# Final norm of token tiles 2 and 3: product and row scaling in one VectorE operation

## The chip, the cores and the metric

The kernel runs on one core of one Trainium2 chip. The metric is the device time of one execution in microseconds; the median of several executions is compared. The core has five engines with a queue of instructions each: TensorE (PE, matmuls), VectorE (DVE), ScalarE (ACT), GpSimd (POOL) and SyncE (SP, which here only issues DMA transfers). ScalarE and GpSimd issue transfers too. An engine runs its queue in order and waits where an instruction needs another engine's result.

## The reference

One layer of a decoder block on 512 tokens with a width of 1024: conditioning from `c`, a combined input projection, two mixers, their merge, a SwiGLU feed-forward layer, and a last RMS norm. All in fp32. The end of it, which the change touches:

```
    h2 = rms_norm(x, norm2_g) * (1.0 + scale2) + shift2
    f_g, f_u = jnp.split(h2 @ w_ffn_in, 2, axis=-1)
    x = x + gate2 * ((jax.nn.silu(f_g) * f_u) @ w_ffn_out)
    return rms_norm(x, final_norm_g)

def rms_norm(x, g):
    y = x * lax.rsqrt(jnp.mean(x * x, axis=-1, keepdims=True) + EPS)
    return y * g
```

## The kernel before

The 512 tokens are four tiles of 128 rows, `xt[0]` to `xt[3]` (`xr` in the profile), with 1024 columns each. Instructions are written out in the order in which each engine runs them; the compiler adds the waits. So the order of the lines is the order of every queue.

The last matrix product, of the gated activations with `w_ffn_out`, is computed by a Strassen-like scheme: seven products of half-size blocks are accumulated in PSUM banks (`pfo`). `zprod` (L1751) runs one such product over six chunks of weights. For each chunk, `get` (L144) first prepares the chunk two ahead: ScalarE copies the raw weights to a rounded high part (`hi`, L112), VectorE subtracts it to get the low part (`lo`, L116), and SP loads a further chunk (L92). Then come the side tasks given for the chunk, then TensorE's matmuls, three for each pair of blocks (L53 to L55).

When the sums of a block of tokens are complete, it is added to the residual stream. `resid_v` (L1234) multiplies a PSUM bank by the gate (`rt`, L1238), adds it to `xt` (L1239), and returns a function that squares the result on ScalarE and accumulates the squares of each row into `ss2` (L1240). In the kernel before, `res_` (L1818) follows this with `scale_g` (L1724), a VectorE product of the new columns of `xt` with the gain vector `fng` into `xo` (L1730).

The last product in time gives tiles 0 and 1, so tiles 2 and 3 are complete earlier. Their three remaining blocks of 512 columns are added during the first three chunks of `zprod(1, "S4", ...)` (L1834). In between stand the weight splits for the last three chunks. Then `done(2)` and `done(3)` finish those rows:

- `row_rstd` (L1246): VectorE adds up the row's squares (L1247), GpSimd raises the sum to the power -1/2 (L1248), into the column `r2[:, tk]` (`sm` in the profile);
- `finish` (L1732): ScalarE scales the last 384 columns of `xo` by that column (L1733), VectorE the first 640 (L1734), and ScalarE and SP each issue a transfer of their part to the output.

After that comes the loop over tiles 0 and 1 (L1842): 15 matmuls for tile 0, twice 15 of half width for tile 1, each followed by residual add, product with the gain, sum, power, scaling and output. The last row's sum is taken in another way (L1864 to L1867). A copy of half a bank on ScalarE (L1836) precedes the loop.

Of the kernel before, what the change touches and what calls it, by code (L numbers as in the profile page):

```python
# [12 lines left out]
AF = mybir.ActivationFunctionType  # L13
OP = mybir.AluOpType
# [3 lines left out]
D = 1024  # L18
# [10 lines left out]
def block_kernel(ctx: ExitStack, tc: tile.TileContext, x, positions, w_ada, b_ada, w_in,  # L29
# [3 lines left out]
    T, V, A, P, SY = nc.tensor, nc.vector, nc.scalar, nc.gpsimd, nc.sync  # L33
# [4 lines left out]
    x, out = x[0], out[0]  # L38
# [3 lines left out]
    def bank(k, name="bank"):  # L42
        return psum.tile([128, 512], F32, name=name, tag=f"b{k}", bufs=1)
# [100 lines left out]
    def get(i, ahead=2):  # L144
        k = wseq.index(i)
        ensure(wseq[min(k + ahead, len(wseq) - 1)])
        return chunk[i]
# [180 lines left out]
    xt = []  # L328
# [903 lines left out]
    r2 = sm[:, 16:20]  # L1232

    def resid_v(p, c0, n, slot, tk, gate):  # L1234

        cs_ = slice(c0, c0 + n)
        t = t512("rt")
        V.tensor_mul(t[:, :n], p, gate[:, cs_])  # L1238
        V.tensor_add(xt[tk][:, cs_], xt[tk][:, cs_], t[:, :n])  # L1239
        return lambda: A.activation(t[:, :n], xt[tk][:, cs_], AF.Square, scale=1.0 / 32,  # L1240
                                    accum_out=ss2[:, tk, slot:slot + 1])
# [4 lines left out]
    def row_rstd(tk):  # L1246
        V.tensor_reduce(r2[:, tk:tk + 1], ss2[:, tk], op=OP.add, axis=AX.X)  # L1247
        P.tensor_tensor(r2[:, tk:tk + 1], r2[:, tk:tk + 1], mhalf[:, :1], op=OP.pow)  # L1248
# [393 lines left out]
    for q in range(-2, NQ):  # L1642
        g, u = 2 + q // 2, q % 2
# [78 lines left out]
    xo = []  # L1722

    def scale_g(c0, n, tk):  # L1724
        if not xo:
            for k in range(2):
                t = ffn[0].tile([128, 2, D], F32, name="xo", tag=f"E{k + 1}", bufs=1)
                xo.extend((t[:, 0], t[:, 1]))
        cs_ = slice(c0, c0 + n)
        V.tensor_mul(xo[tk][:, cs_], xt[tk][:, cs_], fng[0][:, cs_])  # L1730

    def finish(tk):  # L1732
        A.activation(xo[tk][:, 640:], xo[tk][:, 640:], AF.Copy, scale=r2[:, tk:tk + 1])  # L1733
        V.tensor_scalar(xo[tk][:, :640], xo[tk][:, :640], r2[:, tk:tk + 1], None, op0=OP.mult)  # L1734
        for c, q in ((slice(0, 640), SY), (slice(640, 1024), A)):
            q.dma_start(out[tk * 128:(tk + 1) * 128, c], xo[tk][:, c])
# [4 lines left out]
    def zmm(o, ka, c, e, w, cc, start, stop):  # L1741
        ah, al = za[ka, c // 2 if c < 5 else 3]
        wh, wl = w
        for j in range(1 + (c < 5)):
            k_ = 2 * (c % 2) + j if c < 5 else 0
            a = tuple(t[:, k_, e * 128:(e + 1) * 128] for t in (ah, al))
            mm3(o, a, (wh[:, j, cc], wl[:, j, cc]), start and j == 0, stop, skip_group_check=True)
# [3 lines left out]
    def zprod(k, ka, kw, start, tasks):  # L1751
        if start:
            Z[k] = [bank(ZB[k][e], "pfo") for e in range(2)]
        for c, i in enumerate(W_Z[kw][:len(tasks)]):
            w = get(i)
            for fn in tasks[c]:
                fn()
            for e in range(2):
                zmm(Z[k][e], ka, c, e, w, ALL, start and c == 0, c == NZ - 1)
# [29 lines left out]
    fng = []  # L1789
# [25 lines left out]

    sq = []

    def res_(tk, h):  # L1818
        def fn():
            sq.append(resid_v((Z[h] if tk < 2 else Z[2 + h])[tk % 2], 512 * h, 512, h, tk, gate_b[2]))  # L1820
            scale_g(512 * h, 512, tk)
        return fn

    def sq_():
        while sq:
            sq.pop(0)()

    zprod(2, "A22", 4, False, [[res_(0, 0)], [sq_, res_(1, 0)], [sq_], [res_(2, 1)], [sq_, hi_("S4", 3)], [lo_("S4", 3)]])

    def done(tk):  # L1830
        row_rstd(tk)
        finish(tk)

    zprod(1, "S4", (1, 1), False, [[res_(3, 1)], [sq_, res_(2, 0)], [sq_, res_(3, 0)]])  # L1834
    last = bank(7, "pfo")
    A.activation(last[:, :256], Z[1][1][:, 256:], AF.Copy)  # L1836
    ids = W_Z[1, 1][3:]
    ch = [get(i, 2 - k) for k, i in enumerate(ids)]
    sq_()
    done(2)  # L1840
    done(3)
    for tk in range(2):  # L1842
        for z in range(2) if tk else (None,):
            c = ALL if z is None else slice(256 * z, 256 * z + 256)
            o = Z[1][0] if z is None else (Z[1][1][:, :256], last[:, :256])[z]
            for n_, w in enumerate(ch):
                zmm(o, "S4", 3 + n_, tk, w, c, False, n_ == 2)
            n = c.stop - c.start
            if z is None:
                resid(o, 512, 512, 1, tk, gate_b[2])  # L1850
                scale_g(512, 512, tk)
                row_rstd(tk)
            elif z == 0:
                resid(o, 512, n, 1, tk, gate_b[2])
                scale_g(512, n, tk)
                A.activation(xo[0], xo[0], AF.Copy, scale=r2[:, 0:1])
                for c_, q in ((slice(0, 640), SY), (slice(640, 1024), A)):
                    q.dma_start(out[0:128, c_], xo[0][:, c_])

                P.tensor_scalar(ss2[:, tk, 3:4], ss2[:, tk, 1:2], ss2[:, tk, 0:1], EPS, op0=OP.add, op1=OP.add)  # L1860
            else:
                resid_v(o, 768, n, 2, tk, gate_b[2])
                c_ = slice(768, 768 + n)
                V.tensor_tensor_reduce(out=t512("sq")[:, :n], in0=xt[tk][:, c_], in1=xt[tk][:, c_],  # L1864
                                       scale=1.0 / 1024, scalar=ss2[:, tk, 3:4], op0=OP.mult, op1=OP.add,
                                       accum_out=ss2[:, tk, 2:3])
                P.tensor_tensor(r2[:, tk:tk + 1], ss2[:, tk, 2:3], mhalf[:, :1], op=OP.pow)  # L1867
                scale_g(768, n, tk)
                finish(tk)
# [49 lines left out]
```

## Time and profile before

| | us |
|---|---|
| median of 3 runs | 823.59 |
| lowest and highest run | 823.27, 824.55 |
| the profiled execution, its own time | 823.06 |
| span of its instructions | 821.3 |
| TensorE busy | 805.2 (98%) |
| VectorE busy | 688.6 (84%) |
| ScalarE busy | 431.7 (53%) |
| GpSimd busy | 162.3 (20%) |

The span runs from the first to the last instruction; the rest of the execution's time lies around it. Busy times of matmuls overlap, so 98% isn't a measure of how well TensorE is used. TensorE's granted clock was 0.996. A row of the timeline gives start, duration, engine, source line, operation, output and inputs with their shape, and in brackets the idle time before it and what ended it. A row of the chain of waits gives start, duration and the instruction on which the end depends at that moment; "issue" there is time in which the engine waited for nothing that the profile shows.

### The profile page before, as it was taken

Reading aid. Unit: us, or ns where it says so; the run is one execution under the profiler, and the core shown is the slowest. Engines: PE = TensorE matmul, PEld = TensorE weight load, DVE = VectorE, ACT = ScalarE, POOL = GpSimd, SP = SyncE. Lnnn points to the kernel's source line nnn. Section 1 sums busy time; section 2 is a strip of 40 time slices with the busy share of each in tenths; the row PEclk is TensorE's granted clock in tenths of the full one; section 3 lists DMA queues with packets and bytes.
Section 4 is the critical chain, followed back from the end, with each engine's and each line's share of the span. In section 5 each row is a group of like instructions: output and inputs, shape, how many; then the busy total and the mean of one; then the engine's idle time right before and its main releaser. Section 6 shows DMA issues by size and latency. Waiting matters only on the chain.

```text
span 821.3 us, 12948 instructions
## 1 busy us (share of the span) xinstructions
PE 805.2 (98%) x4903; PEld 719.6 (88%) x4903; DVE 688.6 (84%) x1178; ACT 431.7 (53%) x773; POOL 162.3 (20%) x186
## 2 busy tenths in 40 slices
PE   7999999999999999999999999999999999999995
PEld 6889889988888888988888899999999999888874
DVE  7989788898899658887697879889999888897686
ACT  6674445322332226665636586555555556576553
POOL 2060031362354411000010010323121222000001
PEclk9999999999999999999999999999999999999998
DMA  9974352332346553037692603979897977556662
GB/s 294 311 213 119 103 180 78 104 102 86 106 145 204 179 180 103 26 110 256 198 248 43 198 27 117 217 234 275 267 252 208 239 186 192 189 191 202 198 193 113
DMA packets 108462, 141.35 MB, mean 172 GB/s; under 512 B 6688, under 2 KB 77344, under 8 KB 108208
## 3 DMA queue, kind: packets, MB, share of 16 engines
q1 hardware_dynamic: 97296, 110.54, 42.5%
q0 software_dynamic: 10384, 29.17, 15.3%
q8 instruction: 38, 0.62, 0.3%
q10 hardware_dynamic: 720, 0.82, 0.3%
q14 instruction: 24, 0.20, 0.1%
HBM read 138.15 MB, written 25.17 MB: 199 GB/s over the span
## 4 chain that ended last, share of the span: by engine, by line
PE 89%; DVE 5%; DMA 3%; ACT 2%; issue 1%; SPq 0%; POOL 0%; POOLq 0%; ACTq 0%; DVEq 0%
PE pb L53 9%; PE pb L55 9%; PE pb L54 9%; PE R L53 6%; PE R L54 6%; PE R L55 6%; PE pfo L53 4%; PE pfo L55 4%; PE pfo L54 4%; PE pav L54 2%; PE pav L53 2%; PE pav L55 2%; PE pgb L53 2%; PE pgb L54 2%; PE pgb L55 2%; PE po L54 2%
## 5 line engine op out<-in xcount | busy, mean ns | idle before, releaser
L112 ACT ACTIVATE hi<-raw 128x1024 fp32r<-128x1024 f32 (+2 forms) x108 | 109.3, 1013 | 104.0 <-PE pb L54 38.6
L116 DVE TENSOR_TENSOR lo<-raw,hi 128x1024 fp32r<-128x1024 f32 (+2 forms) x72 | 83.5, 1163 | 24.4 <-ACT hi L112 24.1
L116 POOL TENSOR_TENSOR lo<-raw,hi 128x1024 fp32r<-128x1024 f32 x29 | 73.0, 2520 | 127.7 <-ACT hi L112 126.8
L53 PE MATMUL pb<-h,hi 128*128 128x512 f32 (+1 forms) x192 | 74.6, 389 | 0.0
L54 PE MATMUL pb<-h,hi 128*128 128x512 f32 (+1 forms) x192 | 74.0, 385 | 0.0
L55 PE MATMUL pb<-h,lo 128*128 128x512 f32 (+1 forms) x192 | 74.0, 385 | 0.0
L53 PE MATMUL pfo<-hi,za 128*128 128x512 f32 (+1 forms) x144 | 55.9, 388 | 0.3 <-ACT ps L1770 0.3
L55 PE MATMUL pfo<-hi,za 128*128 128x512 f32 (+1 forms) x144 | 55.8, 388 | 0.0
L54 PE MATMUL pfo<-lo,za 128*128 128x512 f32 (+1 forms) x144 | 55.8, 387 | 0.0
L177 DVE SCALAR_TENSOR_TENSOR acc<-mraw,cols,acc 128x512 f32<-128x512 f32 x49 | 40.8, 833 | 17.8 <-DMA mraw<-in_w_ada_dram 16.8
L53 PE MATMUL R<-tb,sx 128*128 128x256 f32 x160 | 45.3, 283 | 0.6 <-ACT R L1689 0.3
L54 PE MATMUL R<-tb,sx 128*128 128x256 f32 x160 | 45.1, 282 | 0.0
L55 PE MATMUL R<-tb,sx 128*128 128x256 f32 x160 | 45.0, 281 | 0.0
L55 PE MATMUL R<-tb,lo 128*128 128x256 f32 x160 | 44.8, 280 | 0.0
L53 PE MATMUL R<-tb,hi 128*128 128x256 f32 x160 | 44.8, 280 | 0.0
L54 PE MATMUL R<-tb,hi 128*128 128x256 f32 x160 | 44.6, 279 | 0.0
L55 PEld LDWEIGHTS pb<-h,lo 128*128 128x128 f32 x192 | 36.0, 187 | 7.3
L54 PEld LDWEIGHTS pb<-h,hi 128*128 128x128 f32 x192 | 36.0, 188 | 6.9
L53 PEld LDWEIGHTS pb<-h,hi 128*128 128x128 f32 x192 | 36.0, 188 | 6.9
L322 POOL COPY sm<-sm 128x1 f32<-128x1 f32 x36 | 23.1, 641 | 86.3 <-ACT sm L321 86.3
L54 PE MATMUL pav<-lo,h 128*128 128x256 f32 x128 | 35.8, 279 | 0.0
L302 POOL DMA_DIRECT2D wsum<-in_w_ffn_out_dram x24 | 21.3, 888 | 73.3 <-DMA wsum<-wsum 42.2
(385 smaller groups left out, 2657.8 us busy)
## 6 DMA issues: line engine op xcount, KB each, us to landing
raw<-in_w_ffn_in_dram SPq DMA_DIRECT2D x44, 512.0 KB, 6.0
raw<-in_w_in_dram SPq DMA_DIRECT2D x40, 512.0 KB, 3.6
wsum<-in_w_ffn_out_dram POOLq DMA_DIRECT2D x30, 512.0 KB, 8.8
mraw<-in_w_ada_dram SPq DMA_DIRECT2D x28, 512.0 KB, 3.8
raw<-wsum SPq DMA_DIRECT2D x20, 512.0 KB, 3.7
raw<-in_w_ffn_out_dram SPq DMA_DIRECT2D x16, 512.0 KB, 4.2
s<-in_w_ada_dram SPq DMA_DIRECT2D x30, 256.0 KB, 5.5
wsum<-wsum POOLq DMA_DIRECT2D x10, 512.0 KB, 5.2
```

What stands on the lines that cost most here:

```text
L53: T.matmul(o, wh, rh, start=start, stop=False, **kw)
L54: T.matmul(o, wh, rlo, start=False, stop=False, **kw)
L55: T.matmul(o, wlo, rh, start=False, stop=stop, **kw)
L112: A.activation(hi[:, :m], e["raw"][:, :m], AF.Copy)
L116: e["lo"].tensor_sub(lo[:, :m], e["raw"][:, :m], f(hi[:, :m]))
L177: V.scalar_tensor_tensor(o, w, cs[:, j:j + 1], o, op0=OP.mult, op1=OP.add)
L302: P.dma_start(wsum[n][o], src, accum_op=OP.add)
L322: P.tensor_copy(t, t)
```

## The change

It concerns tiles 2 and 3 only. For the one block of tile 2 and the two blocks of tile 3 that are added during the last product, the product with the gain vector right after the residual add is left out. After the last weight split both rows' sums and powers are asked for, one after the other. Then a new function, `scaled`, finishes each tile: VectorE multiplies `xt` by the row's column and by the gain vector in one operation, 512 columns for tile 2 and 1024 for tile 3. The other 512 columns of tile 2 have their product already, and ScalarE scales them. Each tile goes out in two transfers of 512 columns, one from SP and one from ScalarE. Tiles 0 and 1 are finished as before.

```diff
+    def scaled(tk, n):
+
+        if n < D:
+            A.activation(xo[tk][:, n:], xo[tk][:, n:], AF.Copy, scale=r2[:, tk:tk + 1])
+        V.scalar_tensor_tensor(xo[tk][:, :n], xt[tk][:, :n], r2[:, tk:tk + 1], fng[0][:, :n],
+                               op0=OP.mult, op1=OP.mult)
+        for c, q in ((slice(0, 512), SY), (slice(512, D), A)):
+            q.dma_start(out[tk * 128:(tk + 1) * 128, c], xo[tk][:, c])
+
...
-    def res_(tk, h):
+    def res_(tk, h, g=True):
         def fn():
             sq.append(resid_v((Z[h] if tk < 2 else Z[2 + h])[tk % 2], 512 * h, 512, h, tk, gate_b[2]))
-            scale_g(512 * h, 512, tk)
+            if g:
+                scale_g(512 * h, 512, tk)
         return fn
...
-    def done(tk):
-        row_rstd(tk)
-        finish(tk)
-
-    zprod(1, "S4", (1, 1), False, [[res_(3, 1)], [sq_, res_(2, 0)], [sq_, res_(3, 0)]])
+    zprod(1, "S4", (1, 1), False, [[res_(3, 1, False)], [sq_, res_(2, 0, False)], [sq_, res_(3, 0, False)]])
     last = bank(7, "pfo")
     A.activation(last[:, :256], Z[1][1][:, 256:], AF.Copy)
     ids = W_Z[1, 1][3:]
     ch = [get(i, 2 - k) for k, i in enumerate(ids)]
     sq_()
-    done(2)
-    done(3)
+    row_rstd(2)
+    row_rstd(3)
+    scaled(2, 512)
+    scaled(3, D)
```

## The prediction

> **What bounds the kernel now.** I read the profile's page first, then the chain of waits from 795 us on, then the timeline engine by engine for the same stretch.
>
> ```profile
> span 821.3 us, 12948 instructions
> PE 89%; DVE 5%; DMA 3%; ACT 2%; issue 1%; SPq 0%; POOL 0%; POOLq 0%; ACTq 0%; DVEq 0%
> ...
> 796.27 0.04 DVE lo L116
> ...
> 816.35 0.61 ACT xo L1733
> ```
>
> TensorE carries 89% of the chain, but the chain leaves it before the end. From 796.27 us to the last scaling at 816.35 us the chain names VectorE, with short visits to GpSimd and ScalarE. So what the changed operations cost VectorE there counts in full, unless something else is late next. These are VectorE's instructions (start, duration) in that stretch:
>
> ```profile
> 799.60 0.69 DVE L1239 TENSOR_TENSOR xr<-xr,rt 128x512 f32<-128x512 f32 x1
> 800.33 0.69 DVE L1730 TENSOR_TENSOR xo<-xr,fng 128x512 f32<-128x512 f32 x1
> 800.94 1.22 DVE L116 TENSOR_TENSOR lo<-raw,hi 128x1024 fp32r<-128x1024 f32 x1
> 802.08 0.69 DVE L1238 TENSOR_TENSOR rt<-pfo,gate2b 128x512 f32<-128x512 f32 x1
> 802.80 0.69 DVE L1239 TENSOR_TENSOR xr<-xr,rt 128x512 f32<-128x512 f32 x1
> 803.53 0.69 DVE L1730 TENSOR_TENSOR xo<-xr,fng 128x512 f32<-128x512 f32 x1
> 804.13 1.22 DVE L116 TENSOR_TENSOR lo<-raw,hi 128x1024 fp32r<-128x1024 f32 x1
> ...
> 806.72 0.69 DVE L1730 TENSOR_TENSOR xo<-xr,fng 128x512 f32<-128x512 f32 x1
> 807.32 0.69 DVE L116 TENSOR_TENSOR lo<-raw,hi 128x512 fp32r<-128x512 f32 x1
> 807.92 0.15 DVE L1247 TENSOR_REDUCE sm<-ss 128x1 f32<-128x5 f32 x1
> 808.76 0.55 DVE L1734 TENSOR_SCALAR xo<-xo,sm 128x640 f32<-128x640 f32 x1 [0.68 <-POOL sm L1248]
> 809.23 0.15 DVE L1247 TENSOR_REDUCE sm<-ss 128x1 f32<-128x5 f32 x1
> 810.05 0.55 DVE L1734 TENSOR_SCALAR xo<-xo,sm 128x640 f32<-128x640 f32 x1 [0.67 <-POOL sm L1248]
> 810.51 0.69 DVE L1238 TENSOR_TENSOR rt<-pfo,gate2b 128x512 f32<-128x512 f32 x1
> ...
> 814.04 0.42 DVE L1238 TENSOR_TENSOR rt<-pfo,gate2b 128x256 f32<-128x256 f32 x1
> ```
>
> There are two things to see. Three L1730 products for tiles 3, 2 and 3 stand between the residual adds and the next weight split. And from 807.92 to 810.51 us the two rows are finished one after the other, with 0.68 and 0.67 us of idle waiting for a power on GpSimd. Everything behind 810.51 us belongs to tiles 0 and 1 and is the same in both kernels. So the question is when that L1238 starts in the changed kernel.
>
> The rows give the steps. A 128x512 product holds VectorE 0.61 us before an independent instruction starts (800.33 to 800.94) and 0.72 us before one that needs its result (802.08 to 802.80). A 1024 split holds it 1.14 us (800.94 to 802.08), the 512 split 0.60 (807.32 to 807.92). A power starts 0.24 us after its sum starts (808.16 below, less 807.92), and its reader 0.60 us after that (808.76).
>
> **Part one: the three products that go.** They are worth 0.61 + 0.60 + 0.60 = 1.81 us on VectorE. Not all of it arrives, because each L116 split also needs ScalarE's copy of the same chunk:
>
> ```profile
> 799.29 1.06 ACT L112 ACTIVATE hi<-raw 128x1024 fp32r<-128x1024 f32 x1 [1.69 <-PE pfo L55]
> ...
> 802.14 1.06 ACT L112 ACTIVATE hi<-raw 128x1024 fp32r<-128x1024 f32 x1 [1.09 <-PE pfo L55]
> ...
> 805.17 0.62 ACT L112 ACTIVATE hi<-raw 128x512 fp32r<-128x512 f32 x1
> 806.72 0.64 ACT L1240 ACTIVATE rt<-xr 128x512 f32<-128x512 f32 x1 [0.92 <-DVE xr L1239]
> 807.25 0.18 ACT L1240 ACTIVATION_READ_ACCUMULATOR rt<-xr 128x1 f32 x1
> ```
>
> The first two of these copies wait for TensorE to release a buffer, and the third stands behind a copy of a product. The change doesn't move TensorE there, so I leave all three in place. I allow 0.02 us from a copy's end to the split.
> - First split: VectorE free at 799.60 + 0.61 = 800.21, copy done at 800.35, start 800.37. Then L1238 at 801.51, L1239 at 802.23, free at 802.84.
> - Second split: copy done at 803.20, start 803.22. Then L1238 at 804.36, L1239 at 805.08 (done 805.77), free at 805.69.
> - Third split: copy done at 805.79, start 805.81, and the first row sum at 806.41 instead of 807.92.
>
> That is 1.51 us earlier; 0.30 of the 1.81 us turns into waits for ScalarE.
>
> **Part two: the new finish.** The second row's sum needs tile 3's last square. That starts when ScalarE is through with the copy, at 805.81, and its accumulator is read 0.53 + 0.18 = 0.71 us later, at 806.52. So this sum can start about 806.55, right behind the first. Both powers are then queued on GpSimd. The only place where two of them ran back to back is the second normalisation:
>
> ```profile
> 468.07 1.41 POOL L1248 TENSOR_TENSOR sm<-sm,mhalf 128x1 f32<-128x1 f32 x2 [34.49 <-DVE sm L1247]
> 468.69 0.75 DVE L1262 TENSOR_SCALAR xn<-xr,sm 128x1024 f32<-128x1024 f32 x1 [0.37 <-POOL sm L1248]
> ...
> 808.16 0.56 POOL L1248 TENSOR_TENSOR sm<-sm,mhalf 128x1 f32<-128x1 f32 x1 [51.27 <-DVE sm L1247]
> ...
> 815.47 0.42 DVE L1730 TENSOR_TENSOR xo<-xr,fng 128x256 f32<-128x256 f32 x1
> 815.64 0.67 POOL L1867 TENSOR_TENSOR sm<-ss,mhalf 128x1 f32<-128x1 f32 x1 [1.02 <-DVE ss L1864]
> ```
>
> A power alone takes 0.56 us; the pair took 1.41, the second half of it beside a VectorE operation that the first power had released. That is just the situation here, so I take 1.41. The lower end is two lone powers, 1.12; the upper end is a second power that finishes only 0.42 us after the VectorE operation beside it, as the one at 815.64 did (815.64 + 0.67 = 816.31, against 815.89).
>
> [...]
>
> The added operations have a tensor, a column and a second tensor as inputs. Their prices come from other lines with that form:
>
> ```profile
> L701 DVE SCALAR_TENSOR_TENSOR sco<-rl,wi,sco 128x512 f32<-128x512 f32 x8 | 6.0, 752 | 1.9 <-ACT rl L698 1.4
> ...
> 168.64 6.72 POOL L116 TENSOR_TENSOR lo<-raw,hi 128x1024 fp32r<-128x1024 f32 x2
> ...
> 169.85 3.27 DVE L906 SCALAR_TENSOR_TENSOR vg<-vg,sm,lnb 128x1024 f32<-128x1024 f32 x1
> ...
> 176.48 1.28 DVE L906 SCALAR_TENSOR_TENSOR vg<-vg,sm,lnb 128x1024 f32<-128x1024 f32 x1
> 177.68 1.28 DVE L905 SCALAR_TENSOR_TENSOR vg<-vg,mva,lng 128x1024 f32<-128x1024 f32 x1
> ```
>
> So 0.75 us for 512 columns, 1.28 for 1024, and 1.20 until the next one starts. The 3.27 us stands beside a long GpSimd operation. GpSimd has nothing here but the power, so I take 1.28 and keep 3.27 as a bound.
>
> The sum, then: first sum 806.41, first power 806.65, first scaling 807.25 (VectorE free about 807.92). The pair of powers ends at 806.65 + 1.41 = 808.06; its reader starts 0.04 later (808.16 + 0.56 = 808.72, against 808.76), so the second scaling starts at 808.10. The next L1238 starts at 808.10 + 1.20 = 809.30 instead of 810.51, a gain of 1.21 us. The finish itself thus becomes longer, 2.89 us from first sum to next L1238 against 2.59 before: the one idle of 0.67 us that goes is less than what 1536 columns in one rate cost over 1280.
>
> **Part three: what else is moved.** Is anything late next?
>
> ```profile
> 808.40 0.39 PE L55 MATMUL pfo<-hi,zl 128*128 128x512 f32 x1
> ...
> 812.05 0.28 PE L55 MATMUL pfo<-hi,zl 128*128 128x256 f32 x1
> ...
> 810.69 0.35 ACTq L1736 DMA_DIRECT2D out_dram<-xo  x1
> ...
> 814.11 1.13 ACT L1856 ACTIVATE xo<-xo,sm 128x1024 f32<-128x1024 f32 x1
> ...
> 816.93 0.33 SPq L1736 DMA_DIRECT2D out_dram<-xo  x1
> ```
>
> TensorE: tile 0's product is done at 808.79, before 809.30. The last product ends at 812.33 and its L1238 would move from 814.04 to 812.83, so 0.50 us of cover is left; a gain over 1.71 us would run into it. ScalarE: two scalings of 384 columns become one of 512, at most 1.13 us by the 1024 row, so done by 808.38. Its second transfer now waits for VectorE's second scaling (808.10 + 1.28 = 809.38) with tile 0's square queued behind it. The issue ends about 809.74; that square can't start before 809.30 + 0.72 + 0.69 = 810.71, so it loses nothing. SP issues the two other halves earlier than now, and its last issue at 816.93 moves with the chain. With 512 columns each the transfers carry as many bytes as before.
>
> So the span goes from 821.3 to about 820.1 us and the profiled execution from 823.06 to 821.85. That execution lies 0.53 below the median of the runs, 823.59; I take the gain off the median: 822.38, rounded 822.4, or 0.15% less. About 0.2% (1.65 us) is what a measurement of this kernel can tell from no change, so this counts as the same.
>
> **The rivals.**
> - The second power is held out (the upper end above). It ends at 807.25 + 0.75 + 0.42 = 808.42, the second scaling starts at 808.46, L1238 at 809.66: gain 0.85, 822.74. For it: the 0.67 us row. Against it: in the pair at 468.07 the second power, too, had a VectorE operation beside it, and ended by 469.48 with that ending at 469.44. Chance 16%.
> - The power is not disturbed at all: the second scaling is set by VectorE, 807.92, L1238 at 809.12: gain 1.39, 822.2. Chance 8%.
> - ScalarE's copies don't hold up the splits (their buffers come free earlier than the waits suggest): another 0.30, gain 1.51, 822.08. Against it: two idle times that end on TensorE. Chance 5%.
> - The change doesn't do what it says: the second sum and power still run only behind the first scaling. Then 807.92 + 0.24 + 0.60 = 808.76 for the second, L1238 at 809.96: gain 0.55, 823.04. In the built program the two sums stand together, which speaks against it. Chance 4%.
> - Slower: the 1024 scaling is as slow as the 3.27 us row. It adds 1.99 us and turns 1.21 of gain into 0.78 of loss: 824.37. It decides from the point where the scalings cost 1.21 us over their rows. Chance 4%.
> - [...] Chance 3%. [...]
>
> **How the numbers follow.** The forecast gets the remaining 60%. The three runs shown lie 1.28 us apart, so a median can wander by some 0.4 us. The range reaches from 822.08 less that wander, 821.6, to 823.2, just above the case of 823.04. It leaves out the two slow cases (7%) and the ends of the wander. Faster by over 0.2% needs 0.44 us of luck on top of the forecast (a sixth of its 60%) or half of the two better cases: 0.18. Slower by over 0.2% needs a slow case and luck, or something that I don't see: 0.05. The rest, 0.77, is the same.
>
> **What would show it.** In the profile of the changed kernel: splits at about 800.4, 803.2 and 805.8 us with idle ended by ScalarE; the two sums within 0.2 us of each other; a second power of about 0.85 us; scalings of 0.75 and 1.28 us; L1238 of tile 0 at 809.3 and the same 10.8 us from there to the end of the span. I'm wrong if a scaling takes 2 us or more, if the second power starts only behind the first scaling, or if the L1238s for tiles 0 and 1 wait for TensorE or ScalarE's queue.

## The result, and the profile after

| | before | changed |
|---|---|---|
| median of 15 runs, us | 823.59 | 821.73 |
| lowest and highest | 822.83, 825.86 | 820.94, 823.29 |
| profiled execution, us | 823.06 | 823.29 |
| its span, us | 821.3 | 821.5 |

The ratio of changed to before is 0.9976, with a 95% interval of 0.9968 to 0.9984: between 1.3 and 2.6 us faster. Timed a second time beside the first experiments it was 0.9981 (0.9972 to 0.9989).

The span of the profiled execution is not shorter, and a reader who compares the two spans would conclude that nothing was gained. That execution happened to be the slowest of the 15 runs. The same instruction, ScalarE's first square of a residual row, stands in the timelines of the kernel before and of the changed one like this:

```profile
461.73 0.63 ACT L1240 ACTIVATE rt<-xr 128x512 f32<-128x512 f32 x1 [2.62 <-DVE xr L1239]
```

```profile
463.77 0.64 ACT L1240 ACTIVATE rt<-xr 128x512 f32<-128x512 f32 x1 [2.62 <-DVE xr L1239]
```

The changed kernel's execution is 2.04 us behind here, 340 us ahead of the first instruction that the change touches. So I read the end of each trace from a mark of its own: ScalarE's copy of half a bank, released by TensorE just ahead of the loop over tiles 0 and 1. The kernel before, then the changed one:

```profile
804.89 0.37 ACT L1836 ACTIVATE pfo<-pfo 128x256 f32<-128x256 f32 x1 [0.64 <-PE pfo L55]
```

```profile
806.50 0.37 ACT L1842 ACTIVATE pfo<-pfo 128x256 f32<-128x256 f32 x1 [1.00 <-PE pfo L55]
```

From that mark to the end of the span it is 821.3 - 804.89 = 16.41 us before and 821.5 - 806.50 = 15.00 us after: 1.41 us less. An earlier mark, ScalarE's first copy of the last product that waits for TensorE (795.18 before, 796.78 after), gives 26.12 and 24.72 us, 1.40 less. VectorE's timeline of the changed kernel answers to the one in the prediction:

```profile
801.21 0.69 DVE L1239 TENSOR_TENSOR xr<-xr,rt 128x512 f32<-128x512 f32 x1
802.18 1.23 DVE L116 TENSOR_TENSOR lo<-raw,hi 128x1024 fp32r<-128x1024 f32 x1 [0.28 <-ACT hi L112]
803.33 0.68 DVE L1238 TENSOR_TENSOR rt<-pfo,gate2b 128x512 f32<-128x512 f32 x1
804.04 0.69 DVE L1239 TENSOR_TENSOR xr<-xr,rt 128x512 f32<-128x512 f32 x1
804.84 1.23 DVE L116 TENSOR_TENSOR lo<-raw,hi 128x1024 fp32r<-128x1024 f32 x1
...
807.43 0.69 DVE L116 TENSOR_TENSOR lo<-raw,hi 128x512 fp32r<-128x512 f32 x1
808.04 0.36 DVE L1247 TENSOR_REDUCE sm<-ss 128x1 f32<-128x5 f32 x2
808.87 1.95 DVE L1736 SCALAR_TENSOR_TENSOR xo<-xr,sm,fng 128x512 f32<-128x512 f32 x2 [0.47 <-POOL sm L1248]
810.74 0.68 DVE L1238 TENSOR_TENSOR rt<-pfo,gate2b 128x512 f32<-128x512 f32 x1
```

The products between the adds and the splits are gone, the two sums stand together (x2 in one row), and so do the two scalings, 1.95 us over both. The chain of waits of the changed kernel shows what took VectorE's place in front of them:

```profile
805.99 0.23 PE pfo L54
806.23 0.25 PE pfo L55
806.47 0.02 issue
806.50 0.02 ACT pfo L1842
806.52 0.26 issue
806.78 0.63 ACT hi L112
807.41 0.02 issue
807.43 0.69 DVE lo L116
808.12 0.08 DVE sm L1247
808.20 0.07 issue
808.28 0.57 POOL sm L1248
808.85 0.03 issue
808.87 1.95 DVE xo L1736 x2
810.82 0.61 DVE rt L1238
```

Before, the chain left TensorE at 795 us. Now it stays with TensorE until 806.47 us, goes through ScalarE's copies to the last split, and only then to VectorE.

### The profile page after: what moved, and what is told of

Its sections match the earlier page's. It is cut to its first block, busy times and chain, and to the rows that moved or that the text cites. A ratio compares the mean times of both kernels' runs of the same rounds, so it can differ in the third digit from the quotient of the medians.

```text
span 821.5 us, 12945 instructions
## 1 busy us (share of the span) xinstructions
PE 805.9 (98%) x4903; PEld 719.6 (88%) x4903; DVE 686.6 (84%) x1175; ACT 430.9 (52%) x772; POOL 166.6 (20%) x186
## 4 chain that ended last, share of the span: by engine, by line
PE 79%; DMA 7%; DVE 7%; ACT 4%; issue 1%; SPq 1%; POOL 0%; POOLq 0%; ACTq 0%; DVEq 0%
PE R L53 8%; PE R L54 8%; PE R L55 8%; PE pb L53 6%; PE pb L54 6%; PE pb L55 6%; PE pfo L53 4%; PE pfo L55 4%; PE pfo L54 4%; DMA mraw<-in_w_ada_dram 3%; PE pav L54 2%; PE pav L53 2%; PE pav L55 2%; DMA s<-in_w_ada_dram 2%; DMA oraw<-in_w_out_dram 2%; PE pgb L53 2%
## 5 line engine op out<-in xcount | busy, mean ns | idle before, releaser
L322 POOL COPY sm<-sm 128x1 f32<-128x1 f32 x36 | 26.0, 723 | 93.7 <-ACT sm L321 93.7
```

The lines of the kernel that those rows point to most:

```text
L322: P.tensor_copy(t, t)
```

## The experiments

The stretches below run from the half-bank copy to the end of the span. Each is one profiled execution; the ratios are of timed runs, with their intervals. extra, nofin and long were timed once only, so they have no ratio.

| kernel | copy, us | span, us | stretch, us | ratio to before |
|---|---|---|---|---|
| before | 804.89 | 821.3 | 16.41 | |
| changed | 806.50 | 821.5 | 15.00 | 0.9976 (0.9968 to 0.9984) |
| again | 804.59 | 820.5 | 15.91 | 0.9981 (0.9972 to 0.9989) |
| serial | 803.69 | 819.5 | 15.81 | 0.9998 (0.9989 to 1.0008) |
| ahead | 804.44 | 820.2 | 15.76 | 0.999 (0.9981 to 0.9999) |
| half | 804.63 | 819.1 | 14.47 | 0.9979 (0.997 to 0.9988) |
| half2 | 804.75 | 819.5 | 14.75 | 0.9972 (0.9959 to 0.9984) |
| extra | 805.85 | 820.9 | 15.05 | |
| nofin | 804.69 | 819.0 | 14.31 | |

**again**: the changed kernel, with no edit.

> The changed kernel itself, timed once more. In the two profiles, the time from the start of ScalarE's copy of half a bank (the last copy before the loop over tiles 0 and 1) to the end of the span is 821.3 - 804.89 = 16.41 us in the kernel before and 821.5 - 806.50 = 15.00 us in the changed one. Theory (VectorE's queue in the finish): 15.0 us again, 1.4 us under the kernel before, ratio 0.998. Rival (chance placement upstream made the profile or the runs): a ratio nearer to 1 or below 0.996, and a stretch that differs from 15.0 by over 0.3 us.

The ratio came as expected, the stretch didn't: 15.91 us. The chain of waits of this run shows why:

```profile
797.55 0.11 DVE zl L1589
797.66 5.13 DMA raw<-in_w_ffn_out_dram
802.79 0.02 issue
802.81 0.04 ACTq L112
802.85 0.04 issue
802.89 1.07 ACT hi L112
803.97 0.02 issue
803.99 1.23 DVE lo L116
```

The load of a chunk of weights took 5.13 us here, and the second of the three splits waited for ScalarE's copy behind it. Against the half-bank copy this split starts 803.99 - 804.59 = -0.60 us here and 804.84 - 806.50 = -1.66 us in the first profile, 1.06 us later. The mark itself holds: TensorE's last matmul starts 811.27 - 804.59 = 6.68 us behind the copy here, as in the first profile (813.18 - 806.50). So in the changed kernel the weight loads are close behind: an execution with a late load lost 0.91 us of the 1.41. In the first profile a load already ended ScalarE's wait ahead of the first split:

```profile
801.09 1.06 ACT L112 ACTIVATE hi<-raw 128x1024 fp32r<-128x1024 f32 x1 [1.88 <-DMA raw<-in_w_ffn_out_dram]
```

How often a load comes late the runs don't tell. The late one was issued 0.44 us later against the copy than in the first profile (797.66 - 804.59 = -6.93, 799.13 - 806.50 = -7.37); the rest is its length, 5.13 us against 4.2 from issue to landing in the first profile, and the cause of that isn't shown. By the letter of the expectation a stretch so far from 15.0 us speaks for chance. One profile of the changed kernel is thus no measure of the whole gain; the two timed sets are, and both show it.

**serial**: the new scaling, with each row's power asked for only ahead of its own scaling.

```diff
     row_rstd(2)
-    row_rstd(3)
     scaled(2, 512)
+    row_rstd(3)
     scaled(3, D)
```

> Changed kernel, but with each row's sum and power asked for only in front of its own scaling (sum 2, scaling 2, sum 3, scaling 3). Theory (the order of the powers is worth a wait of its own): second sum 0.67 us after the first scaling starts, power 0.24 and scaling 0.60 later, so the stretch from the half-bank copy to the end is 15.84 us, 0.84 over the changed kernel and 0.57 under the kernel before. Rival (the three products left out carry the gain, and the power is covered by VectorE's queue): 15.0 us.

15.81 us, against 15.84 expected. The timeline of VectorE shows the second wait for GpSimd back in its place:

```profile
805.24 0.15 DVE L1247 TENSOR_REDUCE sm<-ss 128x1 f32<-128x5 f32 x1
806.07 0.75 DVE L1736 SCALAR_TENSOR_TENSOR xo<-xr,sm,fng 128x512 f32<-128x512 f32 x1 [0.68 <-POOL sm L1248]
806.74 0.15 DVE L1247 TENSOR_REDUCE sm<-ss 128x1 f32<-128x5 f32 x1
807.55 1.29 DVE L1736 SCALAR_TENSOR_TENSOR xo<-xr,sm,fng 128x1024 f32<-128x1024 f32 x1 [0.66 <-POOL sm L1248]
808.75 0.68 DVE L1238 TENSOR_TENSOR rt<-pfo,gate2b 128x512 f32<-128x512 f32 x1
```

The first sum stands 805.24 - 803.69 = 1.55 us behind the copy, as in the changed kernel (1.54), so the two executions differ only from there on. So leaving out the products, the longer scalings included, is worth 16.41 - 15.81 = 0.60 us alone, and the order of the powers 0.81 us on top. The timed runs of serial agree with 0.60 us and with no gain at all. Beside it in the same set the changed kernel's median was 821.19 us against 822.70 for serial, so the order counts in timed runs too. The rival (15.0 us in the trace) falls.

**ahead**: the kernel before, with both sums and powers asked for ahead, the old products and the old finish.

```diff
-    done(2)
-    done(3)
+    row_rstd(2)
+    row_rstd(3)
+    finish(2)
+    finish(3)
```

> Kernel before, with all products with the gain vector and the old finish, but with both rows' sums and powers asked for ahead of both finishes. Theory: VectorE reaches the first sum as late as in the kernel before (3.03 us after the half-bank copy). If the second power runs undisturbed beside the 640-column scaling, the stretch to the end is 15.61 us, 0.80 under the kernel before; if that scaling holds the power out as in the pair at 468 us (1.41 us for two), it is 15.94 us, 0.47 under it. Rival (asking ahead is the whole gain): 15.0 us.

15.76 us, 0.65 under before, between the two values of the theory. Taken in this order, asking ahead is worth 0.65 us alone and the products with the new scaling 15.76 - 15.00 = 0.76 on top, so the parts of the 1.41 us depend on which is taken first. GpSimd's two powers, in the changed kernel and in this one:

```profile
808.28 1.08 POOL L1248 TENSOR_TENSOR sm<-sm,mhalf 128x1 f32<-128x1 f32 x2 [49.78 <-DVE sm L1247]
```

```profile
807.72 1.18 POOL L1248 TENSOR_TENSOR sm<-sm,mhalf 128x1 f32<-128x1 f32 x2 [51.27 <-DVE sm L1247]
```

The pair ends at 808.90 here. VectorE's first scaling beside it, of 640 columns, starts at 808.31 and takes 0.55 us as in the kernel before, so it ends at 808.86. The second power seems to end 0.04 us behind the scaling, as in the pair of the second normalisation. That led to the next experiment.

**long**: like ahead, but VectorE scales all 1024 columns of tiles 2 and 3.

```diff
-    finish(2)
-    finish(3)
+    for tk in (2, 3):
+        V.tensor_scalar(xo[tk], xo[tk], r2[:, tk:tk + 1], None, op0=OP.mult)
+        for c, q in ((slice(0, 640), SY), (slice(640, 1024), A)):
+            q.dma_start(out[tk * 128:(tk + 1) * 128, c], xo[tk][:, c])
```

> Like the kernel with powers asked ahead and the old finish, but VectorE scales all 1024 columns of tiles 2 and 3 itself (ScalarE's part falls away). Theory (a scaling with one tensor input holds the second power back until it ends, one with two tensor inputs doesn't: the two powers took 1.18 us beside the 640-column scaling, 1.08 beside the new operation): the two powers take 0.60 + 0.75 + 0.04 = 1.39 us. Rival (no holding back; 1.18 is scatter): 1.1 to 1.2 us again.

GpSimd's timeline:

```profile
808.19 1.38 POOL L1248 TENSOR_TENSOR sm<-sm,mhalf 128x1 f32<-128x1 f32 x2 [51.77 <-DVE sm L1247]
```

1.38 us against 1.39 expected. The longer scaling with one tensor input holds the second power back further; the new operation, with two tensor inputs and 0.75 us long, didn't at all (1.08 us, in all five profiles with this pair). In each of these pairs the first power releases the scaling, and the second power starts just ahead of it: by an estimate from a lone power of 0.56 us at 808.84, 808.28 and 808.75 in changed, ahead and long, against scalings from 808.87, 808.31 and 808.78. Powers that started while a VectorE operation was already running are another matter. Beside the two-input product of the prediction (815.47, power 0.67 us, the same in all ten profiles) one ended 0.42 us after that product, and beside a one-input scaling in the kernel before another did much the same:

```profile
484.41 0.74 DVE L1262 TENSOR_SCALAR xn<-xr,sm 128x1024 f32<-128x1024 f32 x1
```

```profile
484.57 0.99 POOL L1248 TENSOR_TENSOR sm<-sm,mhalf 128x1 f32<-128x1 f32 x1 [0.33 <-DVE sm L1247]
```

That power ends 485.56 - 485.15 = 0.41 us after the scaling. But a third one in the kernel before, 0.17 us behind tile 1's product with the gate (`pfo` and `gate2b` as inputs), took no longer than alone:

```profile
812.79 0.41 DVE L1238 TENSOR_TENSOR rt<-pfo,gate2b 128x256 f32<-128x256 f32 x1
```

```profile
812.96 0.55 POOL L1248 TENSOR_TENSOR sm<-sm,mhalf 128x1 f32<-128x1 f32 x1 [2.94 <-DVE sm L1247]
```

So in these profiles it counts which operation stands beside the power. Whether the order of the starts counts as well isn't shown: no run changes it alone. The stretch of long, 821.1 - 804.42 = 16.68 us, isn't used: in this execution, too, loads came late ahead of the finish (2.35 and 1.43 us of idle on ScalarE).

**half** and **half2**: tile 3 finished like tile 2, half of its product made early and that half scaled by ScalarE.

```diff
-    zprod(1, "S4", (1, 1), False, [[res_(3, 1, False)], [sq_, res_(2, 0, False)], [sq_, res_(3, 0, False)]])
+    zprod(1, "S4", (1, 1), False, [[res_(3, 1)], [sq_, res_(2, 0, False)], [sq_, res_(3, 0, False)]])
...
-    scaled(3, D)
+    scaled(3, 512)
```

> Changed kernel, but tile 3 is finished like tile 2: the product with the gain vector for its last 512 columns is put back behind their residual add, ScalarE scales them, and VectorE's one-operation scaling of tile 3 has 512 columns. Theory (in the changed kernel VectorE waits for ScalarE's copies, which wait for TensorE, so the product that is put back fits into idle time): the last split is at most 0.1 us later, the scaling 0.53 us shorter, the stretch from the half-bank copy to the end 14.5 us, 0.5 under the changed kernel. Rival (VectorE's work still sets the pace through the splits): the product costs its full 0.61 us, 15.1 us, no gain.

> Tile 3 finished like tile 2, timed again beside the others of this call. Theory: 1.93 us under the kernel before by the chain of the first run (25 to 26 us from ScalarE's first copy of the last product that waits for TensorE to the end: 26.12 before, 24.72 changed, 24.19 here), ratio 0.9977. Rival (the put-back product costs what it saves): 1.4 us, 0.9983. The interval is expected to hold both; the chain tells them apart.

14.47 us, as expected: the product that is put back fits into idle time. In the repeat it was 14.75 us, with a load late again (4.90 us) on its chain. By the chain this version is 0.5 us faster than the changed kernel; the timed runs (0.9979 and 0.9972 against 0.9976 and 0.9981) can't tell the two apart.

**extra**: the same product put back into the changed kernel, for nothing, since the scaling of 1024 columns writes over it.

```diff
-    zprod(1, "S4", (1, 1), False, [[res_(3, 1, False)], [sq_, res_(2, 0, False)], [sq_, res_(3, 0, False)]])
+    zprod(1, "S4", (1, 1), False, [[res_(3, 1)], [sq_, res_(2, 0, False)], [sq_, res_(3, 0, False)]])
```

> Changed kernel with one product more: the product of tile 3's last 512 columns with the gain vector is put back behind their residual add, and VectorE's scaling of 1024 columns writes over it. Theory (that stretch holds idle time ended by ScalarE's copies): the first row sum is at most 0.15 us later against the half-bank copy (1.54 us in the changed kernel), the stretch to the end 15.0 to 15.15 us. Rival (VectorE sets the pace): 2.15 and 15.6 us.

The stretch is 15.05 us, and the first sum starts 1.58 us behind the copy instead of 1.54. A whole product of 0.69 us costs 0.04 here: after the change VectorE no longer sets the pace ahead of the last split. The idle time is then used up: in extra the last split starts at 806.82, just when VectorE is through with the add (806.21 + 0.61).

**nofin**: the sums, powers and scalings of tiles 2 and 3 left out.

```diff
-    row_rstd(2)
-    row_rstd(3)
-    scaled(2, 512)
-    scaled(3, D)
+    for tk in (2, 3):
+        for c, q in ((slice(0, 512), SY), (slice(512, D), A)):
+            q.dma_start(out[tk * 128:(tk + 1) * 128, c], xt[tk][:, c])
```

> Changed kernel without the finish of tiles 2 and 3: their sums, powers and scalings are left out and the unscaled rows are sent out. What remains is what TensorE sets. Theory (TensorE is late next): tile 0's residual product on VectorE starts at the end of its matmuls, 3.4 us after the half-bank copy, the last one for tile 1 within 0.1 us of the last matmul's end, and the stretch to the end is 14.2 us, 0.8 under the changed kernel. Rival (VectorE's queue stays the only bound): 3.4 - 1.9 = 1.5 us, and 12.3 us to the end.

14.31 us against 14.2. VectorE's and TensorE's timelines:

```profile
808.14 0.69 DVE L1238 TENSOR_TENSOR rt<-pfo,gate2b 128x512 f32<-128x512 f32 x1 [1.82 <-PE pfo L55]
...
811.73 0.41 DVE L1238 TENSOR_TENSOR rt<-pfo,gate2b 128x256 f32<-128x256 f32 x1
```

```profile
811.37 0.28 PE L55 MATMUL pfo<-hi,zl 128*128 128x256 f32 x1
```

With the whole finish gone VectorE waits 1.82 us for tile 0's matmuls, and its last product with the gate starts 0.08 us behind the end of TensorE's last matmul (811.65). No idle time stands in front of that product, so there VectorE's queue and TensorE come out level. So of a finish that takes 2.70 us on VectorE in the changed kernel (808.04 to 810.74), only 0.7 us can still be won.

## Why the prediction was right, and where it was off

The time lies in the stated range (821.73, with 821.6 to 823.2), and the mechanism was the one described. The size was off, though: the forecast was 822.4 us, 0.15% faster, and the measured ratio means 0.24%, over the line of 0.2% that I gave a chance of 0.18. The interval, 0.16% to 0.32%, reaches to both sides of that line. Part of the hit is luck: the time lies 0.13 us above the fast end of the range, which has 0.4 us for the wander of a median in it, while the mechanism that the traces show gives 822.2.

- *The three products are worth 1.81 us on VectorE, 1.51 of which reach the first sum.* Against the half-bank copy the first sum came at 807.92 - 804.89 = 3.03 us before and at 808.04 - 806.50 = 1.54 after: 1.49 us. That the rest turns into waits for ScalarE's copies is borne out by the 0.28 us of idle ahead of the first split and by extra. That all three copies stay in place was not quite so: the first waited for a load instead of TensorE, and its split came 0.20 us later against the half-bank copy than forecast (802.18 - 806.50 = -4.32, 800.37 - 804.89 = -4.52). The next two came as forecast.
- *The pair of powers takes 1.41 us.* This is the term that was mis-sized: it took 1.08. I took the row of the second normalisation for "just that situation" because a power ran there beside a VectorE operation. The runs showed that it matters which operation that is: started just behind the second power, a scaling with one tensor input held it back (1.18 us with 640 columns, 1.38 with 1024), the new operation with two inputs didn't. So the case to which I gave 8%, the undisturbed power with a gain of 1.39 us, is what happened; the chain shows 1.41. With the new operation neither side waited: the powers took 1.08 us, and both scalings 1.95, against 0.67 from the first to its successor plus 1.29 in serial, where no power ran beside them. Why a power took 0.67 us behind a two-input product, and a VectorE operation 3.27 beside the long GpSimd operation, isn't shown.
- *The new operation costs 0.75 and 1.28 us.* It took 0.75 and 1.29 in serial. That rules out the case of 3.27 us. No run shows the other of the two slow cases, the one with a chance of 3%: in its place stand 0.75 us for 512 columns and 1.29 for 1024. For each column more the new operation took (1.29 - 0.75) / 512 = 1.05 ns, against (0.75 - 0.55) / 384 = 0.52 ns between the scalings of 640 and 1024 columns with one tensor input. The prediction's rows had that cost in them already.
- *The finish itself becomes longer, 2.89 us against 2.59.* It became 2.70, and the difference from 2.89 is the pair of powers.
- *ScalarE and TensorE are not late.* Right: tile 0's square didn't wait behind the transfers (its 2.58 us of idle end on VectorE's add), and the gain reached the end of the span whole. But TensorE was moved, which the prediction took as fixed: its last matmul starts 812.05 - 804.89 = 7.16 us behind the copy before and 6.68 after, because the last split on VectorE, which TensorE needs, starts 2.43 us behind the copy before and 0.93 after. A matmul at 808.07 waited 0.22 us for it before. That left more cover than the forecast 0.50 us: the last product with the gate starts 0.80 us after TensorE's last matmul ends (814.26 against 813.46).
- *Not foreseen*: that the weight load could come late next. It did on the chains of two profiles (again, half2). In long, which still has the products, a copy waited for a load as well (802.68, 1.43 us of idle), but VectorE was busy until its split could start (804.17, no idle ahead of it).

What stays open is the rest of the size. The chain accounts for 1.41 us. The two timed sets give 1.98 and 1.56 us with intervals that hold 1.41, so nothing more needs a cause, but nothing rules out another half microsecond either.

## What to carry to other kernels

Ask for a small result on a slow path (here a power on GpSimd, 0.84 us from sum to reader) for all rows before the first use, even where the use itself becomes more expensive: the wait was worth 0.81 us of the 1.41 and the merged operation 0.60, or 0.65 and 0.76 taken in the other order. When an engine that bounds a stretch is relieved, price the gain up to the next resource, copy by copy; a product later put back into the freed time cost 0.04 us instead of 0.6. And compare two profiles from a mark near the change: here the spans alone said the opposite of the 15 runs. Such a mark prices a step; for the whole gain it takes the timed runs, since the same kernel gave 15.00 and 15.91 us from the same mark.

## What the runs showed of the hardware

A power on GpSimd that was queued behind another added 0.52 us (1.08 for both) beside the new VectorE operation with two tensor inputs, which started just behind it by the estimate above, and ended with the VectorE operation when that was a scaling with a single tensor input: 1.18 us for both beside 640 columns, 1.38 beside 1024. Of the powers that started while a VectorE operation was already running, two ended about 0.4 us after it, one beside a scaling with one tensor input (0.99 us in all), one beside a product with the gain vector (0.67); a third, beside a product with the gate, took 0.55 as if alone. I had priced all kinds alike.
